# A projection in pairs of columns: masked rows dealt to other pairs, and the weights of pair 3 tied behind a sum of pair 2

## The chip, the cores and the metric

One core of one Trainium2 chip. The metric is the time of one execution on the device in microseconds, the median over runs; beside it stands one profiled execution, from which all rows here come. Its engines: PE (TensorE) multiplies, DVE (VectorE), ACT (ScalarE) and POOL (GpSimd) do element-wise work, SP issues the transfers. Each engine works through its own instructions in order and waits at semaphores for the others.

## The reference

One residual block over x (1 x 2048 x 1024, float32): a norm, one wide input projection, two token mixers side by side, a merge, an output projection. The change lies in the stretch that computes the projection.

```python
h = rms_norm(x, norm_pre_g)
proj = jnp.einsum('bsd,de->bse', h, w_in)              # 1024 columns in, 9232 out
u_a, z_a, q, k, v, o, z_b, gates, g_a, g_b = jnp.split(proj, split_points, axis=-1)
pooled = multiscale_pool(u_a)                          # centred windows 2, 4, 8, 16, minus the token
...
qk = silu(centred_depthwise_conv(concat([q, k]), conv_qk_w, conv_qk_b))
...
mask = jnp.tril(jnp.ones((CHUNK, CHUNK), dtype=bool))  # mLSTM, chunks of 128, two directions
log_d = jnp.where(mask, b[..., :, None] - b[..., None, :] + log_i[..., None, :], -jnp.inf)
...
p_a = jnp.einsum('bsc,cd->bsd', y_a, w_proj_pool)
merged = sigmoid(g_a + b_merge[0]) * p_a + sigmoid(g_b + b_merge[1]) * p_b
return x + rms_norm(jnp.einsum('bsd,de->bse', merged, w_out), norm_post_g)
```

## The kernel before

The projection (`in_pairs`) runs over the two halves of the sequence (1024 tokens each) and, in each, over 36 pairs of 128-column blocks, `i` = 0 to 35. Pairs 0 and 1 are multiplied plainly; from pair 2 on (v pairs apart) a pair is one Strassen product over the four quarters of the tokens' activations (`A11`, `A12`, `A22` and the differences `S1` to `S4`) and of the weights (`B11`, `B21`, `B22` and the differences `T1` to `T4`): seven products instead of eight. To keep float32 accuracy each operand stands as an upper part (`h`, or the first tile) and a lower part (`l`), made by `split`: ACT copies x rounded into the upper part, POOL or DVE subtracts it from x for the lower part (line 105). A product is then three terms times four blocks of the inner dimension, twelve matmuls of 128x512 (`mm3`, lines 113 to 115).

Products gather in three PSUM banks A, B and C. Per pair X, PE's order is: A11·B11 (bankA), S2·T2 (bankB), then A22·T4 and S4·B22 of the pair before, then S1·T1 (bankC), S3·T3 (bankB again) and A12·B21 (bankA). ACT copies bankA to `p1` behind the first. DVE makes `u2` = bankB + p1 (line 476) before S3·T3 may add into the bank, and `u3` = bankB + p1 (line 481) before A22·T4 may. These two sums are `self.read_banks[0]` and `[1]` of the pair. What leaves a bank goes through `raw` (line 706, then a convolution, lines 734 to 745, or window sums, lines 854 to 874) or other outputs, depending on the kind of the pair: pair 2 of half 0 is q, pairs 3 and 4 together are v; in half 1 pair 21 is k, 22 is u, 23 is o, 24 is z, 25 is u.

The weights of pair `i` are prepared while the pair before runs. In half 0 `prep_w` forms t1 to t4 on DVE (line 433) from two loads (`wraw`) and splits them, T2's lower part on DVE, the others on POOL; they are also stored for half 1, where `again_w` loads them (line 396). The code order is only the start: a scheduler that simulates engine times fixes each engine's order, and `tc.high_priority` and `tc.issue_after(x)` (nothing in the block goes ahead of x) shape it. `ties` in half 0 are such bonds for pairs 2 and 3.

In half 1 two side jobs ride along. `masked(u)`, for 32 rows u, loads two slices (line 1110), adds the mask on POOL (line 1114) and stores 256 KB (line 1117): one row in each of the pairs 10 to 33, two in pairs 12, 15, 18, 21, 24, 27, 30 and 33. `split_ahead` loads a piece of `w_proj_pool` (line 1099) into a tile x, splits it (tiles x and hi, called `wp`; upper part on ACT, lower on DVE) and stores both (line 1102), in the pairs of `PRE`. Both jobs take their tiles from one ring:

```python
x, hi = (self.wt_pool.tile([P, 512], F32, tag="wt", name=self.nm("wp")) for _ in range(2))
...
t = self.wt_pool.tile([P, 2, 2, P], F32, tag="wt", name=self.nm("nm"))
```

The ring `wt` holds three tiles; a fourth request waits until the oldest is read out. All transfers named here are issued by SP, in order.

Of the kernel before, what the change touches and what calls it, by code (L numbers as in the profile page):

```python
# [19 lines left out]
NH = 4  # L20
DH = 256
NC_ = S // P
# [14 lines left out]
SI = 3  # L37
LAP = 1
PRE = (4, 5, 7, 9, 10, 16, 17, 19, 20, 22, 24, 25, 27, 29, 32, 33)
FOLDS = (2, 5, 7, 10, 12, 14, 16, 18)  # L40
ROWS = (3, 4, 6, 7, 9)
PB = 2
# [37 lines left out]
def run(steps):  # L80
    for _ in steps:
        pass


class Kernel:
# [62 lines left out]
    def load(self, name, shape, pool=None):  # L148
        t = (pool or self.cpool).tile(shape, F32, tag=name, name=name)
        self.nc.sync.dma_start(t, self.a[name])  # L150
        return t
# [49 lines left out]
    def put(self, H, n, j, x, he, le):  # L201
        return self.split(H[n][0][:, j, :], H[n][1][:, j, :], x, he, le)
# [218 lines left out]
                self.sp[f"wt{i}"][:, k], W[n, "both"].bitcast(F32).rearrange("p a k n -> p a (k n)")  # L421
            )

    def prep_w(self, W, raw, wc, wt):

        nc = self.nc
        b11, b12 = raw[0][:, 0], raw[0][:, 1]
        b21, b22 = raw[1][:, 0], raw[1][:, 1]
        put = lambda n, x, le: self.put_w(W, wc, n, x, le)

        def diff(x, y):
            t = wt.tile([P, 4, P], F32, tag="wt", name=self.nm("wt"))
            nc.vector.tensor_tensor(t, x, y, op=ALU.subtract)  # L433
            return t

        put("B11", b11, "pool")
        if self.edge:
            put("B21", b21, "pool")
        t1 = diff(b12, b11)
        t2 = diff(b22, t1)  # L440
        put("T2", t2, "dve")
        put("T1", t1, "pool")
        t3 = diff(b22, b12)
        put("T3", t3, "pool")
        if not self.edge:
            put("B21", b21, "pool")
        put("T4", diff(b21, t2), "pool")
        put("B22", b22, "pool")
# [69 lines left out]
    def phase1(self):  # L518
        tc, nc, a = self.tc, self.nc, self.a
        with ExitStack() as es:  # L520
# [7 lines left out]
            wc = es.enter_context(tc.tile_pool(name="wc", bufs=10))  # L528
            wt = self.wt_pool = es.enter_context(tc.tile_pool(name="wt", bufs=3))
# [11 lines left out]
            pool = PoolP()  # L541
# [4 lines left out]
            for half in range(2):  # L546
                H = {}
                ops = self.operands(half, H, hp, wc, pool, psum)
                def load(i):
                    return [self.load_w(wr, i, j) for j in range(2)]  # L550

                def work(i, W):
                    return self.pair(half, self.pairs[i], H, W, psum, pool)
# [3 lines left out]
                W = [{}, {}]  # L557
                ahead = lambda: tc.high_priority(offset=NEXT if half else 0)
                with ahead():
                    next(ops)  # L560
                    raw = [self.load_w(wr, i, 0) for i in range(2)]
# [35 lines left out]
                rest, fold = iter(()), self.fold(pool, psum)  # L597
                if half == 0:
                    next(fold)
                for i in range(2, n):  # L600
                    if half == 1 and i == 8:
                        mask = self.decay.tile([P, 2, P], F32, tag="mask", name="mask", bufs=1)
                        nc.sync.dma_start(mask, a["mask"])
                    if half == 0 and i == 8:
                        self.stats(1, pool)
                    self.edge = i == n - 1
                    W = {}
                    with tc.high_priority(offset=200):
                        if half == 0:
                            ties = [self.scaled[8]] if i == 2 else [self.evac, self.gated] if i == 3 else []  # L610
                            with ExitStack() as behind:
                                for t in ties:
                                    behind.enter_context(tc.issue_after(t.ins))
                                self.prep_w(W, load(i), wc, wt)
                        else:
                            self.again_w(W, i, wr, wc)
                    if half == 1 and i in ROWS:
                        with tc.issue_after(self.read.ins):
                            next(rowmath, None)
                    if half == 1:  # L620
                        with tc.issue_after(self.read.ins):
                            for u in range(max(0, 8 * (i - 10) // 6), max(0, min(32, 8 * (i - 9) // 6))):
                                self.masked(u, mask)
                    if half == 1 and i in PRE:
                        with tc.issue_after(self.read.ins):
                            self.split_ahead(*divmod(PRE.index(i), KT))
                    if half == 0:
                        self.keep_w(W, i)


                    if self.pairs[i][0] == "v":

                        if self.pairs[i][1][1] == 0:
                            first = W
                            run(rest)
                        else:
                            run(work(i, (first, W)))
                        rest = iter(())
                        if half == 0 and i + 1 in FOLDS:
                            next(fold)  # L640
                        continue
                    this, self.read_banks = work(i, W), []
                    next(this)
                    if half == 0 and i == FOLDS[0]:
                        next(fold)
                    next(rest, None)
                    next(this)
                    run(rest)
                    if half == 0 and i in FOLDS[1:]:
                        next(fold)  # L650
                    next(this)
                    rest = this
                    if half == 0 and i + 1 in FOLDS:
                        next(fold)
                    if half == 1 and waits is not None and i >= 7 and self.pairs[i][0] not in "qkuvz":
                        kind, h, raw = waits
                        self.conv(pool, kind, h, 1, raw, HALF - 2, 0, self.read_banks)
                        waits = None
                    elif half == 1 and waits is None and late and i >= 10:
                        with tc.issue_after(self.read.ins):  # L660
                            waits = self.late_load(*late.pop(0))
                run(rest)

    def pair(self, half, pair, H, W, psum, pool):
        kind, j = pair[0], pair[1]
        return getattr(self, "pair_" + {"q": "qk", "k": "qk", "ga": "g", "gb": "g"}.get(kind, kind))(
            half, kind, j, H, W, psum, pool
        )
# [1183 lines left out]
```

## Time and profile before

| | |
|---|---|
| median of 3 runs | 2319.06 us (2318.01 to 2320.4) |
| profiled execution: time, span | 2324.11 us, 2322.3 us |
| mean granted clock of PE | 0.995 |
| busy PE, DVE, POOL, ACT | 98%, 62%, 50%, 38% of the span |
| 80 to 90 us | PE busy 4.55 of 10 us, granted clock 0.81 |
| 1240 to 1250 us | PE busy 1.85 of 10 us, granted clock 0.66 |
| DMA over the span | 564.50 MB, mean 243 GB/s |

The busy time of an engine is the sum of its instructions' times. The clock is the share of the full 2.4 GHz that PE was granted. A timeline row gives start, duration, engine, line, output and inputs (buffer numbers left out), how many alike in a row (x2), and in brackets the idle time before it and what ended that. Lines are those of the kernel before; in the changed kernel lines from 40 on are 1 higher, from 602 on 2, and from 665 on 3.

### The profile page before, as it was taken

The numbers are of one execution on the slowest core, as the hardware profiler recorded it, in microseconds if no ns is written. First come the engines' busy times: TensorE is split into PE (matmuls) and PEld (weight loads), VectorE is DVE, ScalarE is ACT, GpSimd is POOL, SyncE is SP. The second block draws the span as 40 slices with busy tenths as digits, with TensorE's granted clock in tenths as the row PEclk, the third lists the DMA queues.
The fourth block names the chain that finished last, engine by engine and source line by source line (L and its number), as shares of the span: only waits on it lengthen the run. The fifth ranks groups of instructions, "written<-read, shape, count | busy, mean of one in ns | idle before, by whom it ended". The sixth has DMA issues, their size and how long they took to land.

```text
span 2322.3 us, 34037 instructions
## 1 busy us (share of the span) xinstructions
PE 2273.6 (98%) x12091; PEld 1955.6 (84%) x12091; DVE 1434.1 (62%) x2383; ACT 883.6 (38%) x1788; POOL 1165.6 (50%) x898
## 2 busy tenths in 40 slices
PE   7999999999999999999998999999999999999998
PEld 5798888888888798988886888799998888999876
DVE  7656756667764565566656763599887452453365
ACT  6434333433343433233232233477766221111332
POOL 4645555666664533366465663155556241234574
PEclk9999999999999999999999999999999999999999
DMA  5577866656685377878877887787766796687863
GB/s 213 190 273 263 290 222 233 246 209 226 226 290 200 110 236 253 291 242 269 284 275 262 278 303 259 255 267 244 236 200 194 264 310 218 227 272 249 314 204 127
DMA packets 233275, 564.50 MB, mean 243 GB/s; under 512 B 23569, under 2 KB 70801, under 8 KB 233105
## 3 DMA queue, kind: packets, MB, share of 16 engines
q1 hardware_dynamic: 233104, 562.33, 70.1%
q8 instruction: 95, 1.56, 0.3%
q14 instruction: 76, 0.61, 0.1%
HBM read 340.46 MB, written 221.77 MB: 242 GB/s over the span
## 4 chain that ended last, share of the span: by engine, by line
PE 35%; DMA 7%; DVE 4%; issue 2%; POOL 2%; ACT 2%; SPq 1%; POOLq 0%; DVEq 0%; ACTq 0%
PE num L1482 4%; PE pb L1129 2%; PE pb L1130 2%; PE pb L1131 2%; PE paps L1130 2%; PE paps L1131 2%; PE paps L1129 2%; PE bankB L113 2%; PE bankB L115 2%; PE bankB L114 2%; PE cu L1129 1%; DMA ox<-mg 1%; PE cu L1130 1%; PE bankC L114 1%; PE bankC L115 1%
## 5 line engine op out<-in xcount | busy, mean ns | idle before, releaser
L105 POOL TENSOR_TENSOR wB<-wraw,wB 128x512 fp32r<-128x512 f32 x220 | 330.4, 1506 | 326.1 <-ACT wB L101 237.9
L101 ACT ACTIVATE wB<-wraw 128x512 fp32r<-128x512 f32 x224 | 138.9, 626 | 250.4 <-PE bankB L115 126.0
L105 POOL TENSOR_TENSOR wT<-wt,wT 128x512 fp32r<-128x512 f32 x102 | 149.5, 1469 | 120.1 <-ACT wT L101 93.5
L739 DVE SCALAR_TENSOR_TENSOR acc<-raw,conv_w,acc 128x1026 f32<-128x1026 f32 (+1 forms) x96 | 150.3, 1580 | 15.2 <-ACT acc L734 14.4
L1466 POOL TENSOR_TENSOR qs<-q,isc 128x256 f32<-128x256 f32 x120 | 90.0, 754 | 128.7 <-PE num L1482 53.0
L101 ACT ACTIVATE wT<-wt 128x512 fp32r<-128x512 f32 x136 | 85.1, 629 | 160.1 <-PE bankB L115 56.7
L1129 PE MATMUL pb<-oxs,w_proj_mlstm 128*128 128x256 f32 x512 | 144.0, 281 | 1.8 <-DVE sgb L1614 1.2
L1130 PE MATMUL pb<-oxs,w_proj_mlstm 128*128 128x256 f32 x512 | 143.8, 281 | 0.0
L1131 PE MATMUL pb<-oxs,w_proj_mlstm 128*128 128x256 f32 x512 | 143.8, 281 | 0.0
L113 PE MATMUL bankB<-A22h,wT 128*128 128x512 f32 x240 | 94.6, 394 | 10.1 <-DVE u L481 10.1
L1114 POOL TENSOR_TENSOR nm<-nm,mask 128x256 f32<-128x256 f32 x64 | 62.9, 996 | 82.4 <-DMA nm<-negM 59.9
L433 DVE TENSOR_TENSOR wt<-wraw,wt 128x512 f32<-128x512 f32 x68 | 63.4, 932 | 64.2 <-POOL wT L105 45.5
L1129 PE MATMUL paps<-pys,w_proj_pool 128*128 128x512 f32 x256 | 101.0, 395 | 0.0
L1130 PE MATMUL paps<-xa,w_proj_pool 128*128 128x512 f32 x256 | 100.8, 394 | 0.1
L1131 PE MATMUL paps<-pys,w_proj_pool 128*128 128x512 f32 x256 | 100.7, 394 | 0.0
L1615 POOL TENSOR_TENSOR pa<-pa,sgb 128x256 f32<-128x256 f32 x64 | 48.6, 773 | 102.9 <-DVE sgb L1614 66.2
L113 PE MATMUL bankB<-S3h,wT 128*128 128x512 f32 x240 | 94.4, 393 | 5.4 <-DVE u L476 5.4
L476 DVE TENSOR_TENSOR u<-bankB,p 128x512 f32<-128x512 f32 x68 | 46.6, 686 | 83.8 <-PE bankB L115 82.9
L1129 PEld LDWEIGHTS pb<-oxs,w_proj_mlstm 128*128 128x128 f32 x512 | 96.4, 188 | 2.2 <-issue 1.4
L1131 PEld LDWEIGHTS pb<-oxs,w_proj_mlstm 128*128 128x128 f32 x512 | 96.7, 189 | 0.0
L1130 PEld LDWEIGHTS pb<-oxs,w_proj_mlstm 128*128 128x128 f32 x512 | 96.4, 188 | 0.0
L113 PE MATMUL bankA<-A12h,wB 128*128 128x512 f32 x240 | 94.3, 393 | 0.0
(463 smaller groups left out, 7545.5 us busy)
## 6 DMA issues: line engine op xcount, KB each, us to landing
wt<-wT SPq DMA_DIRECT2D x136, 512.0 KB, 4.1
wT<-wt SPq DMA_DIRECT2D x136, 512.0 KB, 6.2
wraw<-in_w_in SPq DMA_DIRECT2D x98, 512.0 KB, 5.2
vh<-vnh SPq DMA_DIRECT2D x16, 516.0 KB, 5.3
vl<-vnl SPq DMA_DIRECT2D x16, 516.0 KB, 6.5
v<-vh SPq DMA_DIRECT2D x16, 516.0 KB, 8.8
v<-vl SPq DMA_DIRECT2D x16, 516.0 KB, 8.4
xT<-in_xT SPq DMA_DIRECT2D x16, 512.0 KB, 6.4
```

Source lines behind the costliest of these rows:

```text
L101: self.upper = nc.scalar.activation(hi, x, AF.Copy)
L105: return eng.tensor_tensor(lo, x, hi.bitcast(F32), op=ALU.subtract)
L113: nc.tensor.matmul(ps, wh, xh, start=start and kt == 0, stop=False, skip_group_check=True)
L114: nc.tensor.matmul(ps, wh, xl, start=False, stop=False, skip_group_check=True)
L115: end = nc.tensor.matmul(ps, wl, xh, start=False, stop=stop and kt == 3, skip_group_check=True)
L433: nc.vector.tensor_tensor(t, x, y, op=ALU.subtract)
L739: nc.vector.scalar_tensor_tensor(acc[:, :n], raw[:, tap : tap + n], self.cw[:, ct, tap : tap + 1], acc[:, :n], op0=ALU.mult, op1=ALU.add,)
L1129: nc.tensor.matmul(ps, wh, xh, start=i == 0, stop=False)
L1130: nc.tensor.matmul(ps, wh, xl, start=False, stop=False)
L1131: nc.tensor.matmul(ps, wl, xh, start=False, stop=i == n)
L1466: nc.gpsimd.tensor_tensor(qs[d], q[:, :, ck], isc[:, d, j % 2, None, :].to_broadcast([P, 2, P]), op=ALU.mult)
L1482: nc.tensor.matmul(pn, qs[d][:, kt, :], state[:, kt, :], start=kt == 0, stop=False)
```

## The change

Three places. The masked rows are dealt from one iterator, one per pair from 10 to 33 and a second one in the pairs of a new list `TWICE`; the doubles at 24, 27 and 33 thereby go to 23, 26 and 28, all others stay. The lower part of T1 of pair 2 in half 0 is computed on DVE instead of POOL. And the weights of pair 3 in half 0 are issued only after the first sum of pair 2 (`self.read_banks[0]`, u2), too.

```diff
@@ -37,6 +37,7 @@
 SI = 3
 LAP = 1
 PRE = (4, 5, 7, 9, 10, 16, 17, 19, 20, 22, 24, 25, 27, 29, 32, 33)
+TWICE = (12, 15, 18, 21, 23, 26, 28, 30)
 FOLDS = (2, 5, 7, 10, 12, 14, 16, 18)
 ROWS = (3, 4, 6, 7, 9)
 PB = 2
@@ -421,7 +422,7 @@
                 self.sp[f"wt{i}"][:, k], W[n, "both"].bitcast(F32).rearrange("p a k n -> p a (k n)")
             )
 
-    def prep_w(self, W, raw, wc, wt):
+    def prep_w(self, W, raw, wc, wt, first):
 
         nc = self.nc
         b11, b12 = raw[0][:, 0], raw[0][:, 1]
@@ -439,7 +440,7 @@
         t1 = diff(b12, b11)
         t2 = diff(b22, t1)
         put("T2", t2, "dve")
-        put("T1", t1, "pool")
+        put("T1", t1, first)
         t3 = diff(b22, b12)
         put("T3", t3, "pool")
         if not self.edge:
@@ -597,6 +598,7 @@
                 rest, fold = iter(()), self.fold(pool, psum)
                 if half == 0:
                     next(fold)
+                rows = iter(range(NH * NC_ // 2))
                 for i in range(2, n):
                     if half == 1 and i == 8:
                         mask = self.decay.tile([P, 2, P], F32, tag="mask", name="mask", bufs=1)
@@ -607,11 +609,11 @@
                     W = {}
                     with tc.high_priority(offset=200):
                         if half == 0:
-                            ties = [self.scaled[8]] if i == 2 else [self.evac, self.gated] if i == 3 else []
+                            ties = [self.scaled[8]] if i == 2 else [self.evac, self.gated, self.read_banks[0]] if i == 3 else []
                             with ExitStack() as behind:
                                 for t in ties:
                                     behind.enter_context(tc.issue_after(t.ins))
-                                self.prep_w(W, load(i), wc, wt)
+                                self.prep_w(W, load(i), wc, wt, "dve" if i == 2 else "pool")
                         else:
                             self.again_w(W, i, wr, wc)
                     if half == 1 and i in ROWS:
@@ -619,8 +621,8 @@
                             next(rowmath, None)
                     if half == 1:
                         with tc.issue_after(self.read.ins):
-                            for u in range(max(0, 8 * (i - 10) // 6), max(0, min(32, 8 * (i - 9) // 6))):
-                                self.masked(u, mask)
+                            for _ in range((10 <= i < 34) + (i in TWICE)):
+                                self.masked(next(rows), mask)
                     if half == 1 and i in PRE:
                         with tc.issue_after(self.read.ins):
                             self.split_ahead(*divmod(PRE.index(i), KT))
@@ -660,6 +662,7 @@
                         with tc.issue_after(self.read.ins):
                             waits = self.late_load(*late.pop(0))
                 run(rest)
+            assert next(rows, None) is None
 
     def pair(self, half, pair, H, W, psum, pool):
         kind, j = pair[0], pair[1]
```

What moves on the engines, at the places where PE waits. First DVE in half 0, around u2 of pair 2. `wt` are the differences t1 to t4 (those from wraw_84 and 85 belong to pair 2, 109 and 110 to pair 3, 123 and 124 to pair 4), `S4l` lower parts of the activations; t4 of pair 2 is the row just ahead of each piece. Before:

```order
L105 TENSOR_TENSOR S4l_81_807<-xT_2_308,S4h_80_806 128x512 x2
L433 TENSOR_TENSOR wt_112_961<-wraw_109_954 128x512
L105 TENSOR_TENSOR S4l_81_807<-xT_4_310,S4h_80_806 128x512 x2
L433 TENSOR_TENSOR wt_113_963<-wraw_110_956,wt_112_961 128x512
L433 TENSOR_TENSOR wt_116_971<-wraw_110_956,wraw_109_954 128x512
L105 TENSOR_TENSOR wT2_114_965<-wt_113_963,wT2_114_965 128x512
L433 TENSOR_TENSOR wt_119_979<-wraw_110_956,wt_113_963 128x512
L433 TENSOR_TENSOR wt_126_1037<-wraw_123_1030 128x512
L476 TENSOR_TENSOR u2_103_893<-bankB_100_865,p1_102_879 128x512
L433 TENSOR_TENSOR wt_127_1039<-wraw_124_1032,wt_126_1037 128x512
L433 TENSOR_TENSOR wt_130_1047<-wraw_124_1032,wraw_123_1030 128x512
L481 TENSOR_TENSOR u3_108_938<-bankB_100_865,p1_102_879 128x512
```

And now:

```order
L106 TENSOR_TENSOR S4l_81_807<-xT_2_308,S4h_80_806 128x512
L106 TENSOR_TENSOR S4l_81_807<-xT_4_310,S4h_80_806 128x512 x2
L477 TENSOR_TENSOR u2_103_893<-bankB_100_865,p1_102_879 128x512
L434 TENSOR_TENSOR wt_112_961<-wraw_109_954 128x512
L434 TENSOR_TENSOR wt_113_963<-wraw_110_956,wt_112_961 128x512
L434 TENSOR_TENSOR wt_116_971<-wraw_110_956,wraw_109_954 128x512
L106 TENSOR_TENSOR wT2_114_965<-wt_113_963,wT2_114_965 128x512
L434 TENSOR_TENSOR wt_119_979<-wraw_110_956,wt_113_963 128x512
L434 TENSOR_TENSOR wt_126_1037<-wraw_123_1030 128x512
L434 TENSOR_TENSOR wt_127_1039<-wraw_124_1032,wt_126_1037 128x512
L434 TENSOR_TENSOR wt_130_1047<-wraw_124_1032,wraw_123_1030 128x512
L482 TENSOR_TENSOR u3_108_938<-bankB_100_865,p1_102_879 128x512
```

u2 (u2_103) has moved from behind pair 3's and the first of pair 4's differences to directly behind t4 and S4 of pair 2. All of pair 3 and three differences of pair 4 stand between u2 and u3 (u3_108) now, where it was the last two of them. T1's lower part (wT1_90) is new on DVE, two rows ahead of t4, and one S4l has moved ahead of t4 with it. On ACT, p1 of pair 2 likewise stands directly behind wB11 of pair 3 now, where T2, T1 and T3 of pair 3 stood between.

Then SP in half 1, where pair 24 is prepared while pair 23 runs: `nm` are masked rows (nm18 and nm19 the stores of rows 18 and 19), `wp` the piece that is split ahead, wt24 the kept weights of pair 24. Before:

```order
L1110 DMA nm_1434_10517<-negM_210 128x256
L1110 DMA nm_1435_10523<-negM_210 128x256 x2
L1099 DMA wp_1436_10529<-in_w_proj_pool 128x512
L951 DMA gB5_141<-gB_1374_10166 128x1024
L745 DMA qT2_78<-acc_1376_10183 128x1022
L750 DMA late_1397_10330<-rawk2_133 128x1024
L401 DMA wraw_1449_10650<-wu3_90 128x2x512
L1117 DMA nm18_196<-nm_1434_10517 128x512
L396 DMA wT2_1428_10502<-wt24_116 128x1024
L1117 DMA nm19_197<-nm_1435_10523 128x512
L396 DMA wT1_1429_10504<-wt24_116 128x1024
```

And now:

```order
L1113 DMA nm_1435_10523<-negM_210 128x256
L1102 DMA wp_1436_10529<-in_w_proj_pool 128x512
L954 DMA gB5_141<-gB_1374_10166 128x1024
L1105 DMA wp_61<-wp_1437_10530 128x512
L1105 DMA wp_61<-wp_1436_10529 128x512
L748 DMA qT2_78<-acc_1376_10183 128x1022
L753 DMA late_1397_10330<-rawk2_133 128x1024
L402 DMA wraw_1449_10650<-wu3_90 128x2x512
L397 DMA wT2_1429_10508<-wt24_116 128x1024
L1120 DMA nm19_197<-nm_1435_10523 128x512
L397 DMA wT1_1430_10510<-wt24_116 128x1024
```

Row 18 is gone from here (its loads and its store now stand in pair 23, the store ahead of T2 of pair 23), and the two stores of `wp` have moved up, ahead of qT2, late, a `wraw` load and T2 of pair 24.

Last, ACT at the same place; p1_1411 before and p1_1412 now are p1 of pair 23, wB11 belongs to pair 24. Before:

```order
L101 ACTIVATE wB22_1406_10351<-wraw_1399_10335 128x512
L101 ACTIVATE wB11_1427_10499<-wraw_1425_10496 128x512
L705 ACTIVATE raw_1389_10226<-bankA_1391_10228 128x512
L470 ACTIVATE p1_1411_10375<-bankA_1408_10360 128x512
L101 ACTIVATE wp_1437_10530<-wp_1436_10529 128x512
L101 ACTIVATE wB21_1431_10508<-wraw_1425_10496 128x512
```

And now:

```order
L102 ACTIVATE wB22_1406_10351<-wraw_1399_10335 128x512
L102 ACTIVATE wp_1437_10530<-wp_1436_10529 128x512
L102 ACTIVATE wB11_1428_10505<-wraw_1426_10502 128x512
L708 ACTIVATE raw_1389_10226<-bankA_1391_10228 128x512
L471 ACTIVATE p1_1412_10381<-bankA_1409_10366 128x512
L102 ACTIVATE wB21_1432_10514<-wraw_1426_10502 128x512
```

The upper part of `wp` has moved from behind p1 to ahead of wB11, raw and p1. On DVE its lower part stands ahead of u2 of pair 23 now, where it stood behind it. In pair 27 it moves ahead of p1 in the same way.

## Rows read from the trace of the kernel before

**Rows 1.** Busy times, and PE's waits (us in total, times, longest).
```profile
PE 2273.6 (98%) x12091; PEld 1955.6 (84%) x12091; DVE 1434.1 (62%) x2383; ACT 883.6 (38%) x1788; POOL 1165.6 (50%) x898
...
PE bankB L113 <- DVE u L481: 11.2, 5, 8.2
```

**Rows 2.** PE's timeline, half 0: start us, us, line, out<-in, idle before.
```profile
72.53 0.39 PE L115 MATMUL bankA<-A11h,wB 128*128 128x512 f32 x1
...
80.79 0.58 PE L113 MATMUL bankC<-S1h,wT 128*128 128x512 f32 x1
...
89.35 0.79 PE L113 MATMUL bankB<-S3h,wT 128*128 128x512 f32 x1 [5.45 <-DVE u L476]
...
93.90 0.39 PE L113 MATMUL bankA<-A12h,wB 128*128 128x512 f32 x1
...
97.95 0.40 PE L113 MATMUL bankB<-A22h,wT 128*128 128x512 f32 x1
```

**Rows 3.** DVE's timeline, half 0, same columns.
```profile
64.88 0.69 DVE L105 TENSOR_TENSOR S2l<-xT,S2h 128x512 fp32r<-128x512 f32 x1
...
72.99 1.76 DVE L433 TENSOR_TENSOR wt<-wraw,wt 128x512 f32<-128x512 f32 x1 [7.43 <-POOL wT L105]
...
88.62 0.68 DVE L476 TENSOR_TENSOR u<-bankB,p 128x512 f32<-128x512 f32 x1
...
90.97 0.69 DVE L433 TENSOR_TENSOR wt<-wraw,wt 128x512 f32<-128x512 f32 x1 [1.67 <-DMA wraw<-in_w_in]
```

**Rows 4.** Timelines of POOL, ACT and SP's queue, half 0.
```profile
54.41 16.04 POOL L105 TENSOR_TENSOR S3l<-xT,S3h 128x512 fp32r<-128x512 f32 x4 [6.26 <-ACT S3h L101]
...
70.42 1.29 POOL L105 TENSOR_TENSOR wB<-wraw,wB 128x512 fp32r<-128x512 f32 x1
...
78.61 0.61 ACT L101 ACTIVATE wB<-wraw 128x512 fp32r<-128x512 f32 x1
...
82.76 1.67 ACT L101 ACTIVATE wT<-wt 128x512 fp32r<-128x512 f32 x3 [3.54 <-DVE wt L433]
...
85.01 0.34 SPq L353 DMA_DIRECT2D wraw<-in_w_in  x1
```

**Rows 5.** PE's timeline, half 1, around pairs 23 and 24.
```profile
1221.36 0.39 PE L113 MATMUL bankB<-A22h,wT 128*128 128x512 f32 x1
...
1229.52 0.39 PE L113 MATMUL bankB<-S3h,wT 128*128 128x512 f32 x1
...
1249.40 0.80 PE L113 MATMUL bankB<-A22h,wT 128*128 128x512 f32 x1 [8.15 <-DVE u L481]
...
1256.91 0.39 PE L113 MATMUL bankC<-S1h,wT 128*128 128x512 f32 x1
```

**Rows 6.** Timelines of ACT, POOL and DVE, same stretch.
```profile
1236.22 0.63 ACT L101 ACTIVATE wp<-wp 128x512 fp32r<-128x512 f32 x1 [13.51 <-DMA wT<-wt]
...
1227.94 1.43 POOL L1114 TENSOR_TENSOR nm<-nm,mask 128x256 f32<-128x256 f32 x2 [0.28 <-DMA nm<-negM]
...
1238.41 1.92 POOL L864 TENSOR_TENSOR win<-raw 128x1038 f32<-128x1038 f32 x1 [7.79 <-DVE raw L706]
...
1220.08 0.68 DVE L481 TENSOR_TENSOR u<-bankB,p 128x512 f32<-128x512 f32 x1
...
1248.67 0.68 DVE L481 TENSOR_TENSOR u<-bankB,p 128x512 f32<-128x512 f32 x1
```

**Rows 7.** SP's queue, same stretch: when a transfer is issued.
```profile
1221.57 0.43 SPq L1099 DMA_DIRECT2D wp<-in_w_proj_pool  x1
...
1227.69 0.48 SPq L1117 DMA_DIRECT2D nm<-nm  x1
...
1228.27 0.85 SPq L396 DMA_DIRECT2D wT<-wt  x1
```

**Rows 8.** Landing: tile wp in the whole run; T2 of pair 24.
```profile
DMA to landing us min/median/max: 2.0/5.3/9.2
...
wT<-wt SPq DMA_DIRECT2D x1, 512.0 KB, 9.0
```

## The prediction

> **What bounds the kernel now.** I read the busy times first: PE works in 98% of the span [rows 1], so a change pays only where PE stands still. The list of what PE waits for, sorted by cost, came next. Its dearest line inside the projection is the wait for `u` of line 481 (the second sum over bankB, here u3): 11.2 us over five times, of which one is 8.2 us [rows 1]. Then I looked at PE's own rows around the longest waits, and there are two.
>
> The first is in half 0, pair 2. The product S1·T1 starts at 80.79 and S3·T3 at 89.35, after 5.45 us idle for `u` of line 476 (the first sum, u2) [rows 2]. One product takes 2.72 us: between the starts at 1221.36 and 1229.52 lie three of them [rows 5]. So S3·T3 could have begun at 83.51 and A12·B21 at 86.23; it began at 93.90 [rows 2]. **7.67 us** are lost: 5.45 idle, the rest matmuls that take longer behind the idle time (the one at 89.35 took 0.79, the one at 93.90 0.39).
>
> The second is in half 1, pair 23. A pair takes seven products, 19.04 us. A22·T4 of pair 22 starts at 1221.36, that of pair 23 could start at 1240.40 and starts at 1249.40 after 8.15 us idle for u3. The first matmul behind it takes 0.80 us where the one at 1221.36 took 0.39 [rows 5], and so on for nine matmuls. S1·T1 starts at 1256.91; S3·T3 a pair earlier starts at 1229.52, so S1·T1 a pair earlier at 1226.80 and 1245.84 was due. **11.07 us** are lost. Both together are 18.74 us, 0.8% of the time.
>
> Who is late? In half 0 u2 runs on DVE at 88.62, behind weight differences of pair 3 and half of pair 4's first one; its other operand p1 is copied by ACT behind a group of three splits of pair 3 that waited 3.54 us for DVE and ended at 84.43 [rows 3, 4]. In half 1 the chain is longer. ACT's split of the projection rows (`wp`, upper part) stands idle 13.51 us until 1236.22 [rows 6]. Rows 18 and 19, x and hi ask for four tiles of a ring of three, so hi gets the tile that row 18 holds until its store, issued at 1227.69, has landed: ACT starts 8.5 us after that issue [rows 6, 7], where the row names another transfer that landed about then. DVE's lower part follows, then `raw`, then POOL's first window sum at 1238.41 (7.79 idle for `raw`), and at the end of the window chain u3 at 1248.67 [rows 6].
>
> **The change, part by part.** *Masked rows.* Of the eight pairs with two rows, 24, 27 and 33 split ahead too; their doubles go to 23, 26 and 28. No load, add or store is added. For pair 24 the order shows ACT's `wp` ahead of p1 and DVE's lower part ahead of u2, where they stood behind; on SP the two loads of row 18 are gone from before `wp`'s load, and `wp`'s two stores moved ahead of `qT`, `late`, a `wraw` load and T2 of pair 24. So the tile is free in time, but p1 and u2 of pair 23 and all those loads now queue behind the landing of x.
>
> When does x land? Its load was issued at 1221.57 [rows 7]; two loads fewer ahead of it, at its own 0.43 each, make 1220.7. The transfers of `wp` took 2.0 to 9.2 us, median 5.3 [rows 8]; this stretch is busy, so I take 6.5: 1227.2, with 5.3 and 9.2 as ends (1226.0 and 1229.9). Behind it ACT does wp, wB11, raw and p1 at about 0.6 each (0.63 for wp [rows 6]) and DVE u2 at 0.68: u2 ends 3.1 us after x, at 1230.3. S3·T3 wants it at 1229.52 [rows 5]: 0.8 us of waiting. Two 0.68 `raw` follow, and POOL's window sum starts after the first. From its start to the end of u3 before is 1238.41 to 1249.35, 10.94 us [rows 6], so u3 ends near 1241.9. T2 of pair 24 is the other candidate: the upper part 0.63, the lower about 0.69 and five issues (two stores, three more) of about 0.5 (0.43 and 0.48 [rows 7]) put it 3.8 us behind x, at 1231.0 instead of 1228.27; landing 9.0 us later [rows 7, 8] gives 1240.0, where S2·T2 wants it at 1240.40 − 2.72 + 0.8 = 1238.5: 1.5 more. u3 is wanted behind S2·T2, at 1242.7 by then, so it adds nothing. Sum: 0.8 + 1.5 = 2.3 us. The early end gives 0 + 1.1, the late end 3.5 + 1.5 = 5.0.
>
> One edge is new in pair 23: the doubled row's two extra adds, 1.43 us for two [rows 6], stand on POOL ahead of the convolution's add, whose store frees what the DVE chain before u3 of pair 22 needs. That u3 ended at 1220.76 and is wanted at 1221.36 [rows 5, 6]: 0.60 us of slack, so 0 to 0.8 us lost; I take 0.4, as DVE's `p` of line 884 now runs earlier. Gain: 11.07 − 2.3 − 0.4 = **8.4** (5.3 to 10.0). In pairs 26 and 28 neither tile ring nor PE is short in the trace; I cost them at nothing, covered by PE's own work. If that cover fails, each extra pair of adds costs its 1.43 us.
>
> *T1's lower part on DVE, and the tie.* POOL loses an operation of 1.29 us (the like of wB11's lower part [rows 4]), DVE gains one of 0.69 (as the one before it [rows 3]). On DVE u2 now stands directly behind t4 of pair 2 and the S4 parts; all of pair 3 comes after it, and on ACT p1 directly behind pair 3's first split. So p1 is at about 79.3 (78.61 + 0.61 [rows 4]), and u2 after t4 (72.99 before, up to 1.3 us later now, 1.76), two S4 parts (as t4, 1.76 each) and itself: 73.0 + 1.3 + 1.8 + 3.5 + 0.7 = 80.3 [rows 3]. Wanted: 83.51. The wait is gone, with 3.2 us to spare.
>
> What is late next is u3 of pair 2. It stands behind two differences of pair 4 (t2, t3), the first of which waited for a weight load until 90.97, issued 5.96 us before at 85.01 [rows 3, 4]. That load now waits for pair 3's third difference: u2's end and three operations, near 83.7, plus 5.96 is 89.7, plus two differences and u3 at 0.68 is 91.8. A22·T4 of pair 2 came 4.05 us behind A12·B21 (93.90 to 97.95 [rows 2]), two small matmuls of 0.12 are put ahead of it, so it wants u3 at 86.23 + 4.05 + 0.24 = 90.5. I take 1.3 us lost; the load may land 3 us later (9.0 is the longest here [rows 8]): 0 to 4.3. Gain: 7.67 − 1.3 = **6.4** (3.4 to 7.7).
>
> One rule speaks against the DVE part. In the trace the first of four S3 parts on POOL, begun at 54.41, takes 16.04 − 3 × 1.29, so 12.2 us; it ends near the end of DVE's close sequence at 65.57 [rows 3, 4]. The Trainium skill, "SBUF — State Buffer", section "Who interferes with whom", says that a VectorE instruction with two SBUF inputs and a GpSimd one that reads SBUF take turns under an exclusive lock, the second being blocked fully. The trace agrees with that. By the rule two more DVE operations right behind 65.57 hold POOL for 1.2 us, and wB11 of pair 2 ends at 72.9, 0.4 us after the third matmul that needs it (72.53 [rows 2]); without it, wB11 ends at 71.71 and nothing is lost. That 0.4 lies inside the 1.3 above, since a later S1·T1 shifts what u3 must meet.
>
> Sum: 8.4 + 6.4 = 14.8 us. The profiled execution took 2324.11 us, 2322.3 of it the span, so it would take 2309.3; the median of the runs is 5.05 us lower, so **2304.3 us**.
>
> **Rivals.** *One stall returns.* If x lands near 9.2 us with T2's load slow as well, or if pair 4's load in half 0 holds u3, one half of the gain goes; the 13.51 us of ACT's wait show how far one tile reaches, while the 3.2 us of spare at u2 speak against half 0. Keeping only half 0's 6.4 gives 2312.7, only half 1's 8.4 gives 2310.7. Take 2308.8 to 2314.4.
>
> *The chain does not shorten.* If the window chain's start were set by something other than `wp`, u3 of pair 23 would still end near 1249 and pair 2's stall would be only shifted from u2 to u3: no change, 2319. Against it: POOL idled 7.79 us for exactly `raw` [rows 6], and DVE's work of pairs 3 and 4 stands straight ahead of u2 in half 0, with PE idle until u2 ends [rows 2, 3].
>
> *Slower.* SP issues in order, and in pair 24 it now stops at `wp`'s first store until x has landed and been split. T2 of pair 24 lands 3.8 + 9.0 behind x, wanted at 1237.68: from x at 1224.9 on, each microsecond is one of PE. To be over 4.6 us slower, this place must lose 11.07 + 6.4 + 4.6 = 22 us, that is x landing at 1247, 26 us after its issue, and the time 2324. The longest transfer of `wp` took 9.2 us [rows 8], and the same hold at 27 and 33 would have to cost as well to come near; little speaks for it.
>
> **How the numbers follow.** The forecast (both stalls mostly gone, 2301.4 to 2310.4 by the ends of the two gains, 17.7 and 8.7 us) has 64%; one stall returning 20%; no change 9%; slower 7%. 4.6 us (0.2%) is about what a measurement of this kernel can tell from no change. The range of all cases runs from 2299.5, just under the ends since both stalls together are 18.74 us, to 2313.0, which takes in most of the second case: about 80%. Faster by over 4.6 us: 0.84, within: 0.09, slower: 0.07.
>
> **What would show it.** PE's waits for lines 481 and 476 fall from 16.6 us to some 4; S3·T3 of pair 2 follows S1·T1 at once; ACT's `wp` of pair 24 comes 8 to 10 us earlier and its idle time is ended by the load of `wp`. A wait of PE at S2·T2 of pair 24 for a weight load, and one at A22·T4 of pair 2, each of 1 to 2 us, would show the two residues. I am wrong if a new wait over 4 us stands at u2 or u3 of pairs 2 or 23, or if pairs 26 to 28 show any.

## The result, and the profile after

The changed kernel took 2306.72 us (2305.99 to 2307.57, six runs) against 2319.73 us before in the same runs: a ratio of 0.9943, 95% interval 0.9933 to 0.9952, so 13.0 us less (11 to 15.5). In a later set of runs the same kernel stood at 2309.42 against 2319.45, ratio 0.9954 (0.9940 to 0.9967), 10.0 us less. One of the eleven runs of the kernel with the tie and T1 alone, below, took 3722 us at a granted clock of 0.57 and does not count in its ratio. The profiled execution of the changed kernel took 2306.88 us with a span of 2305.1.

What PE waits for (us in total, times, longest), changed kernel:

```profile
PE bankB L114 <- DVE u L482: 5.8, 6, 1.6
...
PE bankB L114 <- DVE u L477: 2.2, 1, 2.2
...
PE bankA L116 <- POOL wB L106: 0.3, 1, 0.3
```

Line 482 is line 481 of before, 477 is 476. The two long waits, 8.15 us in [rows 5] and 5.45 us in [rows 2], are gone; 8.3 us of short ones stand in these three lines. Of these 5.5 us are new, at the four places shown next with a wait; the other 2.7 stand at four places where before had 3.1 us. PE's timeline in the changed kernel, half 0 and then pairs 22 to 24 of half 1:

```profile
72.49 0.50 PE L116 MATMUL bankA<-A11h,wB 128*128 128x512 f32 x1 [0.28 <-POOL wB L106]
...
84.07 0.39 PE L114 MATMUL bankB<-S3h,wT 128*128 128x512 f32 x1
...
92.80 0.50 PE L114 MATMUL bankB<-A22h,wT 128*128 128x512 f32 x1 [1.58 <-DVE u L482]
...
1217.51 0.50 PE L114 MATMUL bankB<-A22h,wT 128*128 128x512 f32 x1 [1.47 <-DVE u L482]
...
1236.68 0.39 PE L114 MATMUL bankB<-A22h,wT 128*128 128x512 f32 x1
...
1242.12 0.39 PE L114 MATMUL bankC<-S1h,wT 128*128 128x512 f32 x1
...
1247.18 0.50 PE L114 MATMUL bankB<-S3h,wT 128*128 128x512 f32 x1 [2.18 <-DVE u L477]
```

S3·T3 of pair 2 starts at 84.07 with no wait, where it was 89.35. A22·T4 of pair 2 then waits 1.58 us for u3. In half 1 the 8.15 us at A22·T4 of pair 23 are gone (1236.68, no wait); A22·T4 of pair 22 waits 1.47 us where before it had none, and S3·T3 of pair 24 2.18 us.

The lead of the changed kernel is how much earlier than in before a matmul starts; it is read by laying the same matmul of both traces side by side. At A22·T4 of pair 2 it is 97.95 − 92.80 = 5.15 us; at A22·T4 of pair 22 1221.36 − 1217.51 = 3.85; at S1·T1 of pair 24 1256.91 − 1242.12 = 14.79; the wait behind it takes 2.3 back, so 12.5 us leave the projection. The span is 17.2 us shorter. The other 4.7 come late in the program, where none of the three edits acts, from short waits that this one execution of before happened to have: a second profile of the changed kernel has the same waits in the projection and a span of 2309.1, 4.0 us longer, and one of the waits by which it is longer is this:

```profile
PE pb L1132 <- DVE sgb L1617: 1.2, 1, 1.2
```

So 12.5 us by the trace stand beside 13.0 and 10.0 us by the run times.

DVE, POOL and ACT in half 0 of the changed kernel (start, us, idle time before and what ended it):

```profile
73.72 1.76 DVE L434 TENSOR_TENSOR wt<-wraw,wt 128x512 f32<-128x512 f32 x1 [7.41 <-POOL wT L106]
...
75.40 2.98 DVE L106 TENSOR_TENSOR S4l<-xT,S4h 128x512 fp32r<-128x512 f32 x3
...
81.71 0.69 DVE L477 TENSOR_TENSOR u<-bankB,p 128x512 f32<-128x512 f32 x1 [3.33 <-DMA sga<-sg]
...
90.59 0.96 DVE L434 TENSOR_TENSOR wt<-wraw,wt 128x512 f32<-128x512 f32 x1 [0.75 <-DMA wraw<-in_w_in]
...
92.07 0.68 DVE L482 TENSOR_TENSOR u<-bankB,p 128x512 f32<-128x512 f32 x1
...
53.95 17.24 POOL L106 TENSOR_TENSOR S3l<-xT,S3h 128x512 fp32r<-128x512 f32 x4 [6.26 <-ACT S3h L102]
...
71.16 1.28 POOL L106 TENSOR_TENSOR wB<-wraw,wB 128x512 fp32r<-128x512 f32 x1
...
79.85 0.57 ACT L471 ACTIVATE p<-bankA 128x512 f32<-128x512 f32 x1
```

p1 of pair 2 is copied at 79.85 and ends at 80.42; u2 runs at 81.71, held until then by a store of `sga` and no longer by the weights of pairs 3 and 4; PE wants it at 84.07. u3 ends at 92.75, directly behind two differences of pair 4, the first of which waited for its load until 90.59. The first S3 part on POOL takes 17.24 − 3 × 1.29 = 13.4 us, 1.2 more than in [rows 4].

The same in half 1, with SP's issues:

```profile
1199.05 3.12 POOL L1117 TENSOR_TENSOR nm<-nm,mask 128x256 f32<-128x256 f32 x3
...
1202.13 2.40 POOL L747 TENSOR_TENSOR acc<-acc,raw 128x1026 f32<-128x1026 f32 x1
...
1225.78 1.91 POOL L867 TENSOR_TENSOR win<-raw 128x1038 f32<-128x1038 f32 x1
...
1208.47 1.24 ACT L737 ACTIVATE acc<-late,conv_b,conv_w 128x1022 f32<-128x1022 f32 x1 [7.14 <-DMA kT<-acc]
...
1219.94 0.63 ACT L102 ACTIVATE wp<-wp 128x512 fp32r<-128x512 f32 x1 [1.43 <-DMA wp<-in_w_proj_pool]
...
1239.12 0.63 ACT L102 ACTIVATE wp<-wp 128x512 fp32r<-128x512 f32 x1 [9.77 <-DMA pooled<-pooled]
...
1216.77 0.68 DVE L482 TENSOR_TENSOR u<-bankB,p 128x512 f32<-128x512 f32 x1
...
1223.83 0.68 DVE L477 TENSOR_TENSOR u<-bankB,p 128x512 f32<-128x512 f32 x1
...
1234.48 0.68 DVE L482 TENSOR_TENSOR u<-bankB,p 128x512 f32<-128x512 f32 x1
...
1239.79 1.22 DVE L106 TENSOR_TENSOR wp<-wp,wp 128x512 fp32r<-128x512 f32 x1 [1.18 <-ACT wp L102]
...
1240.94 2.32 DVE L871 SCALAR_TENSOR_TENSOR pooled<-win,raw 128x1032 f32<-128x1032 f32 x1
...
1245.24 1.28 DVE L742 SCALAR_TENSOR_TENSOR acc<-late,conv_w,acc 128x1022 f32<-128x1022 f32 x1 [1.12 <-ACT acc L737]
...
1246.44 0.68 DVE L477 TENSOR_TENSOR u<-bankB,p 128x512 f32<-128x512 f32 x1
...
1214.01 0.84 SPq L1102 DMA_DIRECT2D wp<-in_w_proj_pool  x1
...
1225.15 0.61 SPq L397 DMA_DIRECT2D wT<-wt  x1
...
1231.49 0.33 SPq L1102 DMA_DIRECT2D wp<-in_w_proj_pool  x1
```

ACT's `wp` of pair 24 starts at 1219.94, when its load has landed, 5.9 us after its issue at 1214.01. POOL's first window sum begins 12.6 us earlier than in [rows 6], at 1225.78, and u3 of pair 23 runs at 1234.48 in place of 1248.67; 3.9 us of both differences are the lead that PE already had. What is late now is pair 25's `wp`: its load, issued at 1231.49, took 7.5 us to land, so ACT splits it at 1239.12 (the row names a store of `pooled`), and DVE's lower part at 1239.79 stands ahead of the second window sum, of the convolution's first step (1245.24) and of u2 of pair 24 (1246.44).

At pair 22 the rows of before to hold against these are POOL's add and ACT's first step behind its store:

```profile
1205.67 2.40 POOL L744 TENSOR_TENSOR acc<-acc,raw 128x1026 f32<-128x1026 f32 x1
...
1211.37 1.24 ACT L734 ACTIVATE acc<-late,conv_b,conv_w 128x1022 f32<-128x1022 f32 x1 [5.11 <-DMA kT<-acc]
```

One thing that the prediction read from before can be tested there as well: whether ACT's `wp` of pair 24 waited for a tile of the ring. The load of x landed 8.8 us after its issue, at 1230.4, and the store of row 18 landed 8.3 us after its own (1227.69 [rows 7]), at 1236.0; ACT started at 1236.22, 0.2 us behind the store and 5.9 us behind the load. No kernel with a fourth tile was run.

### The profile page after: what moved, and what is told of

It is laid out like the page before. It is cut to its first block, busy times and chain, and to the rows that moved or that the text cites. A ratio compares the mean times of both kernels' runs of the same rounds, so it can differ in the third digit from the quotient of the medians.

```text
span 2305.1 us, 34033 instructions
## 1 busy us (share of the span) xinstructions
PE 2268.6 (98%) x12091; PEld 1953.0 (85%) x12091; DVE 1439.6 (62%) x2384; ACT 882.7 (38%) x1788; POOL 1167.9 (51%) x897
## 4 chain that ended last, share of the span: by engine, by line
PE 88%; DVE 4%; DMA 3%; issue 2%; ACT 1%; POOL 1%; SPq 0%; DVEq 0%; POOLq 0%; ACTq 0%
PE bankB L114 7%; PE bankB L115 7%; PE bankB L116 7%; PE bankA L114 5%; PE bankA L115 5%; PE bankA L116 5%; PE bankC L115 5%; PE bankC L114 5%; PE bankC L116 5%; PE num L1485 4%; PE pb L1134 3%; PE pb L1132 3%; PE pb L1133 3%; PE paps L1133 3%; PE paps L1132 3%; PE paps L1134 3%
```

## The experiments

Each kernel was run beside the kernel before. The four kernels with a part of the change (rows; tie and T1; tie; T1) shared a chip; so did the changed kernel again, the second row at 31, the split ahead at 26 and the tie of pair 4; and so did T1 back on POOL, the tie of pair 4 again, and the two kernels that combine edits. Times are medians.

**Rows alone.** The changed kernel without the tie and with T1 on POOL:

```diff
-                            ties = [self.scaled[8]] if i == 2 else [self.evac, self.gated, self.read_banks[0]] if i == 3 else []
+                            ties = [self.scaled[8]] if i == 2 else [self.evac, self.gated] if i == 3 else []
...
-                                self.prep_w(W, load(i), wc, wt, "dve" if i == 2 else "pool")
+                                self.prep_w(W, load(i), wc, wt, "pool")
```

> Only the masked rows are dealt anew; half 0 stays as before. Theory (the two edits act in two separate places and add up): PE's 5.45 us idle at S3·T3 of pair 2 stays, the 8.15 us at A22·T4 of pair 23 goes, the new waits of 1.5 us at A22·T4 of pair 22 and 2.2 us at S3·T3 of pair 24 are there, gain 7.1 us (0.31%). Rival (the rows bring most of it, half 0's gain is given back later): 12 to 13 us. Rival (the rows bring nothing by themselves): 0.

Measured: 2314.81 against 2318.97 us, ratio 0.9977 (0.9968 to 0.9985): 0.23% where 0.31% was expected, which the interval just takes in. By the trace the lead at the end of the projection is the 7.1 us expected. PE's rows of this kernel show the wait of half 0 as before:

```profile
89.61 0.80 PE L114 MATMUL bankB<-S3h,wT 128*128 128x512 f32 x1 [5.44 <-DVE u L477]
```

**Tie and T1 alone.** The changed kernel with the rows dealt as before:

```diff
-                            for _ in range((10 <= i < 34) + (i in TWICE)):
-                                self.masked(next(rows), mask)
+                            for u in range(max(0, 8 * (i - 10) // 6), max(0, min(32, 8 * (i - 9) // 6))):
+                                self.masked(u, mask)
```

> Only T1's lower part on DVE and the tie; the masked rows stay 1, 1, 2. Theory (separate and additive): S3·T3 of pair 2 follows S1·T1 without waiting, A22·T4 of pair 2 waits about 1.6 us, the 8 us at A22·T4 of pair 23 stays, gain 5.5 us (0.24%). Rival (given back by pair 23, whose wait depends on transfers and not on PE): 0 to 2 us.

Measured: 2315.15 us, ratio 0.9980 (0.9971 to 0.9989). The stall of pair 23 stays:

```profile
1242.86 0.80 PE L114 MATMUL bankB<-A22h,wT 128*128 128x512 f32 x1 [6.57 <-DVE u L482]
```

It is 6.57 us idle here, 7.09 and 6.74 in the next two kernels, where the one profile of before had 8.15. Waits of 0.81 and 0.39 us at pairs 27 and 32 stand in this profile and in no other of the four. The two gains (0.23% and 0.20%) sum to 0.43%, inside the interval of the second measurement of the whole (0.33 to 0.60%) and just below that of the first (0.48 to 0.67%); the run times alone do not show how exactly they add up. The traces show that neither is given back: the changed kernel leads the one with the rows alone by 5.7 us at A22·T4 of pair 2 (98.49 − 92.80) and still by 5.4 at the last wait of the projection, the rows alone first:

```profile
1468.61 0.50 PE L114 MATMUL bankB<-A22h,wT 128*128 128x512 f32 x1 [0.78 <-DVE u L482]
```

```profile
1463.18 0.50 PE L114 MATMUL bankB<-A22h,wT 128*128 128x512 f32 x1 [0.78 <-DVE u L482]
```

**Tie alone** (rows as before, T1 on POOL; both edits shown above).

> Only the tie of pair 3's weights behind u2 of pair 2; T1's lower part stays on POOL. Theory (the queue ahead of u2 on DVE and of p1 on ACT is the cause): the same 5.5 us as with both, perhaps 0.3 us more, as the wait of 0.28 us of PE at A11·B11 of pair 2 for POOL's wB goes. Rival (POOL's chain to t4 is the cause, and T1 on DVE frees it): under 1 us.

Measured: 2312.56 us, ratio 0.9969 (0.9957 to 0.9981). No wait at S3·T3 of pair 2 and none at A11·B11; PE and DVE of this kernel:

```profile
84.27 0.39 PE L114 MATMUL bankB<-S3h,wT 128*128 128x512 f32 x1
...
93.00 0.50 PE L114 MATMUL bankB<-A22h,wT 128*128 128x512 f32 x1 [1.58 <-DVE u L482]
...
75.20 6.84 DVE L106 TENSOR_TENSOR S4l<-xT,S4h 128x512 fp32r<-128x512 f32 x4
...
81.97 0.68 DVE L477 TENSOR_TENSOR u<-bankB,p 128x512 f32<-128x512 f32 x1
```

u2 runs at 81.97, as in the changed kernel, though the four S4 parts beside a busy POOL take 1.71 us each. That this kernel is faster than the one with T1 moved as well is not shown: the intervals overlap.

**T1 alone** (no tie, rows as before).

> Only T1's lower part of pair 2 on DVE; no tie, rows as before. Theory (order before u2 is the cause): u2 stays behind pair 3's differences, PE waits 5 us at S3·T3 of pair 2 as before, gain 0, or a loss of 0.3 us at A11·B11 of pair 2 because POOL's S3 parts end later. Rival (POOL's chain is the cause): 4 us gain or more.

Measured: 2318.57 us, ratio 0.9996 (0.9988 to 1.0005). PE waits at both places:

```profile
72.87 0.50 PE L116 MATMUL bankA<-A11h,wB 128*128 128x512 f32 x1 [0.28 <-POOL wB L106]
...
88.97 0.80 PE L114 MATMUL bankB<-S3h,wT 128*128 128x512 f32 x1 [4.36 <-DVE u L477]
```

u2 ran at 88.24 behind pair 3's differences. The tie does the work in half 0; T1 on DVE gains nothing that the run times show.

**T1 back on POOL**, rows and tie as changed (the line of `prep_w` above).

> The changed kernel with T1's lower part of pair 2 back on POOL: rows and tie alone. Theory (the tie does the work in half 0; T1 on DVE only costs the 0.28 us at A11·B11 of pair 2): the same time as the changed kernel within 0.6 us, the 0.28 us wait gone, S3·T3 of pair 2 still without a wait, 1.6 us at A22·T4 of pair 2 as there. Rival (T1 on DVE is needed for u2 to be in time): a wait of over 1 us at S3·T3 of pair 2, slower than the changed kernel by that.

Measured: 2308.12 against 2318.54 us, ratio 0.9955 (0.9942 to 0.9969), as the changed kernel. No wait at A11·B11 or S3·T3 of pair 2, 1.57 us at A22·T4. The lower part's move can be left out.

**The changed kernel again.**

> The changed kernel itself once more, to compare the three others with on the same chip: 2306 to 2308 us, with the same waits of PE at A22·T4 of pairs 2 and 22 and S3·T3 of pair 24, 1.5 to 2.2 us each. If these are chance of one execution, they differ by more than 0.5 us here.

Measured: 2309.42 us. The three waits are 1.61, 1.44 and 2.21 us: they are no chance of one execution. The second is less steady from kernel to kernel: it is 0.7 to 1.5 us in kernels that differ from this one only elsewhere.

**The second row of pair 23 moved to 31.**

```diff
-TWICE = (12, 15, 18, 21, 23, 26, 28, 30)
+TWICE = (12, 15, 18, 21, 26, 28, 30, 31)
```

> The changed kernel with the second masked row of pair 23 moved on to pair 31. Theory (the two extra adds of pair 23 on POOL stand ahead of the convolution's add, whose store delays the chain to u3 of pair 22): PE's wait of 1.5 us at A22·T4 of pair 22 falls under 0.3, all else as in the changed kernel, 1.5 us faster than it. Rival (the wait comes from DVE sharing its time with POOL, whatever POOL does): the wait stays at 1 us or more, no difference.

Measured: 2309.01 us, the changed kernel beside it 2309.42. The wait at pair 22 is gone, as the theory said, but the time is not. PE and ACT of this kernel:

```profile
1225.74 0.50 PE L114 MATMUL bankB<-S3h,wT 128*128 128x512 f32 x1 [1.03 <-DVE u L477]
...
1247.78 0.79 PE L114 MATMUL bankB<-S3h,wT 128*128 128x512 f32 x1 [2.70 <-DVE u L477]
...
1211.23 0.63 ACT L948 ACTIVATE gB<-p 128x512 f32<-128x512 f32 x1 [3.27 <-DVE p L887]
...
1222.53 0.63 ACT L102 ACTIVATE wp<-wp 128x512 fp32r<-128x512 f32 x1 [5.96 <-DMA wp<-in_w_proj_pool]
```

With one row in pair 23 the order puts DVE's `p` of line 887 behind two convolution steps again; ACT's next output and split wait for it, and the issue of `wp`'s load behind them on SP comes at 1215.65, 1.6 us later than in the changed kernel. x lands later, u2 of pair 23 is late by 1.03 us, u2 of pair 24 by 2.70. Beside the changed kernel's first profile 1.6 us are won at pair 22, 1.3 lost at S3·T3 of pair 23 and 2.0 at S3·T3 of pair 24 (1.5 of them by slower matmuls behind the wait, see the last section). So the early `p` was worth about as much as the adds cost.

**The split ahead of pair 25 moved to 26** (and the second row of pair 26 to 31).

```diff
-PRE = (4, 5, 7, 9, 10, 16, 17, 19, 20, 22, 24, 25, 27, 29, 32, 33)
-TWICE = (12, 15, 18, 21, 23, 26, 28, 30)
+PRE = (4, 5, 7, 9, 10, 16, 17, 19, 20, 22, 24, 26, 27, 29, 32, 33)
+TWICE = (12, 15, 18, 21, 23, 28, 30, 31)
```

> The changed kernel with the split ahead of pair 25 moved to pair 26 and the second masked row of pair 26 to pair 31. Theory (wp of pair 25 stands on ACT ahead of p1 and on DVE ahead of u2 of pair 24, and waits for its load): PE's wait of 2.2 us at S3·T3 of pair 24 falls under 0.5, 2 us faster than the changed kernel, if pair 26 has room. Rival (the window and convolution chain of pair 24 on DVE is late by itself): the wait stays above 1.5 us, no difference.

Measured: 2309.26 us beside 2309.42. The wait at S3·T3 of pair 24 falls from 2.2 to 0.86 us:

```profile
1246.32 0.50 PE L114 MATMUL bankB<-S3h,wT 128*128 128x512 f32 x1 [0.86 <-DVE u L477]
```

So about 1.3 us of it came from `wp` of pair 25, and 0.9 is the window and convolution chain on DVE, where u2 now stands directly behind the convolution's first step. Two new waits of 0.17 and 0.22 us stand at pairs 27 and 31. The time shows no gain. Beside the changed kernel's profile from the same chip the trace wins 0.75 us at A22·T4 of pair 22, which the edit does not touch, and 1.4 at pair 24; 1.0 of this is lost again in small steps between pairs 25 and 35, and 0.3 late in the program.

**Pair 4 tied behind u3 of pair 2.**

```diff
-... else [self.evac, self.gated, self.read_banks[0]] if i == 3 else []
+... else [self.evac, self.gated, self.read_banks[0]] if i == 3 else [self.read_banks[1]] if i == 4 else []
```

> The changed kernel with the weights of pair 4 tied behind u3 of pair 2 as well. Theory (u3 of pair 2 is late because pair 4's differences, which wait for a weight load, stand ahead of it on DVE): PE's wait of 1.6 us at A22·T4 of pair 2 goes, 1.6 us faster than the changed kernel. Rival (pair 4's weights then come late for the v products): a new wait of 1 us or more there, no difference or slower.

Measured: 2305.86 us, 3.6 under the changed kernel on the same chip (2309.42). u3 on DVE and A22·T4 of pair 2 on PE:

```profile
88.75 0.68 DVE L482 TENSOR_TENSOR u<-bankB,p 128x512 f32<-128x512 f32 x1
...
91.52 0.40 PE L114 MATMUL bankB<-A22h,wT 128*128 128x512 f32 x1
```

The wait is gone, and a wait of 1.1 us at the v products near 220 us as well (in the kernel of all edits below, which has this tie too, 0.6 us of it stand). By the traces the lead over the changed kernel's two profiles is 1.3 and 1.9 us at A22·T4 and 2.5 and 3.4 from the v products to pair 24, which is about what the run times show. In this one profile 1.5 us are lost again at pair 24, where 2.31 us of waiting are followed by slower matmuls (last section).

**That kernel again.**

> The kernel with the tie of pair 4 once more, to compare the others with on the same chip: 13 to 15 us under the kernel before, 2 to 3 us more than the changed kernel gains. If its lead over the changed kernel was chance, it gains 10 to 13 us here.

Measured: 2304.91 against 2318.54 us, ratio 0.9939 (0.9927 to 0.9951): 13.6 us.

**Tie of pair 4 and the split ahead at 26 together.**

> The changed kernel with the tie of pair 4 and with the split ahead of pair 25 moved to 26, the second row of 26 to 31. Theory (the two residues are apart and add up): no wait at A22·T4 of pair 2, 0.9 us instead of 2.2 at S3·T3 of pair 24, 1 to 2 us under the kernel with the tie of pair 4 alone. Rival (given back at pairs 26 to 30): no gain over it.

Measured: 2307.18 us beside 2304.91, ratio 0.9948 (0.9936 to 0.9961). 0.90 us at S3·T3 of pair 24 as expected, but 0.45 and 0.63 us at pairs 31 and 32 are new; it gains nothing over the tie alone. Beside the second profile of that kernel 1.2 us are won at pair 24 and 1.7 lost by pair 32: here the rival, given back at the pairs behind, is what the trace shows.

**All of them** (tie of pair 4, split ahead at 26, T1 on POOL, second rows at 14 and 31 in place of 23 and 26).

> Rows, tie, and the tie of pair 4, T1 on POOL, the second rows of pairs 23 and 26 moved to 14 and 31, the split ahead of pair 25 moved to 26. If the waits at A22·T4 of pair 22 and at S3·T3 of pair 24 have separate causes, both are under 0.9 us and the time is 2 us under the kernel with the tie of pair 4 alone. Rival (as when the second row of 23 was moved alone: DVE's p of pair 21 then stands later, the load of wp of pair 24 too, and u2 of pair 23 waits 1 us): no gain over it.

Measured: 2305.21 us, ratio 0.9938 (0.9926 to 0.9951), level with the tie of pair 4 alone. The 2 us over it that were expected did not come. Its profile has the fewest waits in the projection: beside two that every kernel has, 0.97 us at S3·T3 of pair 24, 0.61 at the v products and none at pairs 2 and 22, a lead of 2.4 us over the other's second profile at the end of the projection, and a span of 2300.4; the medians do not tell the two apart. Each stands some 3 us under the kernel that it can be compared with on its chip, the changed one for the tie of pair 4 (2305.86 to 2309.42) and the rows and the tie alone for this one (2305.21 to 2308.12).

## Why the prediction was right, and where its terms were off

The time forecast, 2304.3 us, stands 2.4 us under the measured one and 5.1 under that of the later set, both inside the range; both stalls went for the reasons given, and the case *both stalls mostly gone* was the one that came. The step from the profile to the median, 5.05 us, held: 4.7 us of the difference between the two profiles lie late in the program. By its steps:

- *u2 of pair 2 in time.* Right. It was put at 80.3 and ended at 82.40, with 1.7 us to spare instead of 3.2, as it waited for a store that the sum did not have. What was ascribed to the two edits together is the tie's alone.
- *u3 of pair 2, the residue.* Right in place and cause (the load of pair 4), 1.3 us forecast, 1.58 idle measured. That the load was issued at 84.42, near the 83.7 put, is in part luck: u2 ended 2.1 us late, and the three differences behind it took 1.9 us where the sum had 3.4; with 0.28 at A11·B11 and the slower first matmuls the stall left about 2.3 us (7.67 less a lead of 5.15 to 5.5). Half 0 gave 5.4 for 6.4.
- *What spoke against T1 on DVE.* POOL's first S3 part took 13.4 us with T1 on DVE and 12.2 with it on POOL (in before and in the tie alone), and wB11 ended at 72.44, so the third matmul of A11·B11 waited 0.28 us, where 0.4 was put. The trace agrees with the rule that the prediction takes from the Trainium skill, "SBUF — State Buffer", section "Who interferes with whom".
- *u3 of pair 22.* The step that allowed 0 to 0.8 us and took 0.4 was too small: 1.47 us idle, 1.6 with the slower matmul behind it. PE's lead before this wait was 5.5 us (S2·T2 of pair 23 starts at 1218.64 in before and at 1213.15 now). With that laid on, POOL's add for the convolution starts 2.0 us later than in before (1205.67 and 1202.13), not 1.4; from its end to ACT's next step, which waits for the store, it is 3.9 us for 3.3; and the way from there to u3 is 0.4 us shorter with the early `p` out of it. That makes 2.2 us, against 0.60 of slack.
- *The landing of x.* Put too late by 2 to 3 us: 1227.2 was said, and 1219.94 plus a lead of 3.9 to 5.5 us is 1223.8 to 1225.4 on before's scale. The issue was earlier (the early `p` let ACT and SP go on) and the landing 5.9 us, not 6.5. So the 2.3 us at u2 of pair 23 and T2 of pair 24 were not lost at all; the second load landed in time too.
- *What is late next.* This is the step that failed: the text followed the stall to u3 of pair 23 and stopped, and costed nothing at u2 of pair 24. There 2.3 us were lost, 1.3 of them behind `wp` of pair 25 (the split ahead at 26 shows it) and the rest behind the window and convolution chain; in before PE's own 8 us of standing still covered both. Half 1 gave 11.07 − 1.6 − 2.3 = about 7.1 us for 8.4.
- *The size of the second stall.* The 11.07 us come from one profile with 8.15 us idle; the three kernels that deal the rows as before had 6.6 to 7.1 there. They differ from before in half 0, so it is not shown, but the stall was probably dearer in that profile than in most runs, as the run times of the rows alone suggest.
- *Pairs 26 to 30 at nothing.* Right: no wait of PE there.
- *What would show it.* PE's waits for the two sums fell from 16.6 to 8.0 us, not to some 4: the difference is pairs 22 and 24. ACT's `wp` came 11 to 12 us earlier on before's scale, for 8 to 10. Of the two residues named, the one at A22·T4 of pair 2 came and the one at S2·T2 of pair 24 did not.
- *The slower rival,* SP stopped at `wp`'s store: T2 of pair 24 was issued at 1225.15, 5.2 us behind the start of the split of x where 3.8 was put, and no product waited for it.

## What to carry to other kernels

When a stall is taken away, walk on from the place where it stood: work that was in time only because the waiting engine stood still is the next to be late, and it is found in the rows right behind the stall. A short instruction that frees a bank for the bound engine belongs ahead of work for later stages on every in-order queue that it uses, here DVE for u2 and ACT for p1; a bond on the later work does that without touching the engines' shares. And a tile ring one short shows as a wait for a store far from the engine that pays.

## What was not expected of the hardware

A wait can cost PE more than its idle time, and two waits of nearly the same length need not cost the same. At S3·T3 of pair 24, from the start of its first matmul to the start of the next product, the changed kernel took 2.90 us behind 2.18 us idle, the rows alone 2.87 behind 2.28, the tie of pair 4 4.44 behind 2.31 in its first profile and 2.85 behind 2.08 in its second, and the second row at 31 4.43 behind 2.70. In the two dear cases six or seven matmuls took 0.63 us each instead of 0.39. In the tie's first profile they are not even the first ones behind the wait, which took 0.50 and 0.39:

```profile
1244.70 0.50 PE L114 MATMUL bankB<-S3h,wT 128*128 128x512 f32 x1 [2.31 <-DVE u L477]
```

The same window of five microseconds (busy times of PE, PE's weight loads, DVE, ACT and POOL, then the granted clock), the changed kernel first, then the second row at 31, then the tie of pair 4:

```profile
1245.00:1250.00 5.00, 2.82 (x12) 2.32 (x13) 4.75 (x5) 1.19 (x4) 0.00 (x0) 1.00 1.01 387
```

```profile
1245.00:1250.00 5.00, 2.30 (x6) 1.82 (x6) 4.16 (x5) 0.81 (x1) 0.00 (x0) 0.78 1.02 381
```

```profile
1245.00:1250.00 5.00, 5.00 (x16) 3.92 (x15) 4.52 (x5) 2.20 (x4) 1.12 (x1) 0.66 0.67 267
```

The first stayed at the full 2.4 GHz; the others, at 0.78 and 0.66 on the mean, ran part of the time at the 1.2 GHz level, which cost 1.5 us beyond the wait. The time of the same program differed by 2.7 us between two sets of runs (2306.72 and 2309.42), as much as some of these edits are worth.
